# Moving a runtime branch ahead of the expert loop, and norms per tile behind it, in a two-layer mixer and mixture-of-experts kernel

## Chip, cores, metric

One core of a Trainium2 chip. The metric is the device time of one execution in microseconds (us).

## What is computed

Two layers over 512 tokens (256 context, 256 latent) of width 1024. Each layer has a token mixer and then a mixture of experts: every token goes to its best group of four and, in it, to the two best of eight experts, 32 experts in all, each a SwiGLU MLP with 256 hidden columns. Around the experts stands a residual with a layer norm, and the next layer begins with a second, plain norm of that result:

```python
for l in range(DEPTH):
    yc, yl = token_mixer(modulate(xc, sh1c, sc1c), modulate(xl, sh1l, sc1l), ...)
    xl = layer_norm(DEEPNORM_ALPHA * xl + g1l * yl, ln1_g[l], ln1_b[l])
    if not last:   # the context stream, in the same way
        xc = layer_norm(DEEPNORM_ALPHA * xc + g2c * hier_moe(modulate(xc, sh2c, sc2c), *moe_args), ln2_g[l], ln2_b[l])
    xl = layer_norm(DEEPNORM_ALPHA * xl + g2l * hier_moe(modulate(xl, sh2l, sc2l), *moe_args), ln2_g[l], ln2_b[l])
```

Layer 0 does this for four tiles of 128 tokens, layer 1 for the two latent tiles alone. The shifts, scales and gates (sh, sc, g) come from a matrix `w_ada` of 1024 x 6144 per layer, which the kernel calls `ada`, in three parts of 2048 columns.

## The kernel before

The kernel is written in a framework that orders the instructions of each engine itself, from a simulated timeline, and places the waits; only TensorE's order inside the expert loop is fixed by hand (`manual_schedule`). A conditional block (`tc.If`) is one unit for the engines that take part in it.

`moe(l)` (L1278 to L1537) runs in this order. `route` finds every token's two experts and how many experts have more than 64 tokens; `route_rows` writes this as rows. Each expert has one block of 64 token places; further blocks, for experts with more tokens, are counted in `cnt`. Experts are taken in pairs: `fetch(j)` finds on VectorE (DVE, `who`) which tokens sit in pair j and gathers their rows from DRAM with an indirect DMA of GpSimd (POOL, `gather`); `turn` transposes them on TensorE (PE); `up`, `hidden` and `down` are the MLP; `combine` puts the results back to the tokens with matmuls by a 0/1 matrix, multiplies by the gate on DVE (L1444) and adds to the residual `X` (L1447), on POOL or DVE.

Expert weights come through a ring of buffers of 1 MB (`wm`: 4 of the pool W and 7 or 9 of the pool W2, and in layer 1 one more), issued by SyncE (SP); a pair takes six.

In layer 0 one further block is computed always, after pair 3 (`extra(0, self.wm)`). For all others there is the branch: `nov` is loaded from `cnt` into registers of PE, ScalarE (ACT), DVE and POOL (L1478), and behind the experts stands a nest of `tc.If(nov > ob)` (L1520), each with an `extra`. With these inputs no engine goes into it in either layer: it is jumped over.

In layer 0 the drain of the last `combine` is followed by `self.drain(self.ada(1, 1, True))`, the second part of the next layer's `ada`, with 16 weight loads of 512 KB through the 4 buffers of pool W alone, then by the branch, then by the norms, in groups of two tiles: `ln_stats` (BATCH_NORM_STATS2 on DVE, L209, and an inverse root by Newton steps, L147 to L154), `affine` (L236, L237), and `ln_scale` for the next layer's norm. Then `mixer(1)` starts: loads of `w_in`, `ada(1, 2)`, and per tile the normalised `xn` (ACT, L486), its transposes (PE, L489), scale and shift `h` (L502, L504), a split into high and low parts (L505, L160), and matmuls (L196 to L198). In layer 1 the branch and the norms of two tiles end the kernel, and the output is stored from L1537.

## Time and profile before

| | us |
|---|---|
| median of 3 runs | 1450.9 (1450.35 to 1451.05) |
| the profiled execution | 1449.59 |
| its span, first to last instruction | 1447.8 |

| engine | busy us | share |
|---|---|---|
| PE (matmul) | 1294.9 | 89% |
| DVE | 800.6 | 55% |
| ACT | 436.4 | 30% |
| POOL | 388.9 | 27% |

The expert loops lie at 542 to 817 us (layer 0) and 1197 to 1425 us (layer 1). Busy time counts an instruction from its start to its end; matmuls are pipelined and their ends are modelled. Idle time in brackets is that of the engine ahead of an instruction, with what ended it. An engine's name with a q is its sequencer: branches, register loads, semaphores, DMA issues.

### The profile page before, as it was taken

What the parts mean: (1) busy time and instruction counts of PE and PEld (TensorE: products, weight loads), DVE (VectorE), ACT (ScalarE), POOL (GpSimd) and SP (SyncE); (2) the same over time, 40 slices, a digit from 0 to 9 for tenths busy, and PEclk for the clock granted to TensorE, in tenths of its full rate; (3) what the DMA queues carried; (4) which work ended last, traced back from release to release, by engine and by line L of the source; (5) the groups of instructions that cost most, each with busy time, mean ns of one, the idle gap of its engine ahead of it and who ended that gap; (6) DMA issues with size and microseconds to landing.
All of it is one profiled execution on the core that took longest, in us unless ns stands there. A gap on an engine that the chain in (4) does not pass through costs nothing. (4 is left out here: it accounts for less than half of the span.)

```text
span 1447.8 us, 19597 instructions
## 1 busy us (share of the span) xinstructions
PE 1294.9 (89%) x6839; PEld 833.9 (58%) x6839; DVE 800.6 (55%) x2205; ACT 436.4 (30%) x976; POOL 388.9 (27%) x395
## 2 busy tenths in 40 slices
PE   5899999999998829899999967999999739999994
PEld 1788866776876623445444405897978633444442
DVE  3646677543246955446653458568775763343325
ACT  3434344443340102112112006355554202221210
POOL 1410114110342303343432412111524401222222
PEclk9899999999999859999999979999999959999997
DMA  9624464211257568979999596412434687999993
GB/s 331 195 95 146 139 207 145 83 30 59 88 182 259 183 241 307 404 274 408 407 407 409 215 304 227 125 44 75 128 127 151 202 290 293 416 417 416 414 417 126
DMA packets 146031, 339.60 MB, mean 235 GB/s; under 512 B 21552, under 2 KB 67792, under 8 KB 145920
## 3 DMA queue, kind: packets, MB, share of 16 engines
q1 hardware_dynamic: 137376, 322.87, 61.0%
q0 software_dynamic: 6096, 10.05, 2.1%
q10 hardware_dynamic: 2448, 5.31, 1.1%
q8 instruction: 57, 0.93, 0.3%
q14 instruction: 54, 0.44, 0.1%
HBM read 344.62 MB, written 4.29 MB: 241 GB/s over the span
## 5 line engine op out<-in xcount | busy, mean ns | idle before, releaser
L1404 PE MATMUL ps_g<-we,xs 128*64 128x512 f32 x992 | 236.7, 604 | 3.1 <-DMA we<-in_w_e_up 3.0
L1447 POOL TENSOR_TENSOR X<-X,acc 128x512 f32<-128x512 f32 x102 | 134.6, 1343 | 111.5 <-DVE acc L1444 111.2
L160 POOL TENSOR_TENSOR wsl<-wc,wsh 128x512 fp32r<-128x512 f32 x55 | 73.6, 1340 | 329.7 <-ACT wsh L176 282.4
L1404 PEld LDWEIGHTS ps_g<-we,xs 128*64 128x64 f32 x992 | 74.5, 139 | 140.7 <-issue 134.9
L176 ACT ACTIVATE wsh<-wc 128x512 fp32r<-128x512 f32 x162 | 99.0, 628 | 152.4 <-PE ps_g L197 83.1
L160 DVE TENSOR_TENSOR wsl<-wc,wsh 128x512 fp32r<-128x512 f32 x107 | 86.8, 815 | 97.6 <-ACT wsh L176 86.4
L1408 DVE SCALAR_TENSOR_TENSOR si<-si,ws,ps_g 128x256 f32<-128x256 f32 (+1 forms) x33 | 15.8, 480 | 206.0 <-ACT si L1407 206.0
L1427 PE MATMUL ps_a<-we,hidT 128*64 128x512 f32 x496 | 124.7, 601 | 3.2 <-DMA we<-in_w_e_down 3.1
L196 PE MATMUL ps_g<-wsh,hTh 128*128 128x256 f32 x400 | 115.8, 292 | 5.9 <-ACT hTh L527 3.1
L1360 POOL DMA_INDIRECT xr<-h2d,ti x33 | 34.7, 1053 | 310.0 <-PE ps_t L1372 204.6
L198 PE MATMUL ps_g<-wsh,hTl 128*128 128x256 f32 x400 | 113.1, 286 | 4.0 <-DVE hTl L160 3.3
L196 PE MATMUL ps_g<-hTh,wsh 128*128 128x512 f32 (+1 forms) x320 | 112.8, 352 | 1.8 <-ACT tg L621 1.8
L197 PE MATMUL ps_g<-wsl,hTh 128*128 128x256 f32 x400 | 114.2, 287 | 0.0
L197 PE MATMUL ps_g<-hTl,wsh 128*128 128x512 f32 (+1 forms) x320 | 111.1, 347 | 0.0
L198 PE MATMUL ps_g<-hTh,wsl 128*128 128x512 f32 (+1 forms) x320 | 110.4, 345 | 0.0
L375 PE MATMUL ps_d<-wada,sT 128*32 128x512 f32 x380 | 76.6, 662 | 31.4 <-DMA wada<-in_w_ada 31.4
L1444 DVE TENSOR_TENSOR acc<-ps_d,g 128x512 f32<-128x512 f32 x108 | 73.9, 688 | 37.8 <-PE ps_d L1442 21.7
L1441 PE MATMUL ps_d<-yh,pmr 128*128 128x512 f32 (+1 forms) x200 | 83.4, 418 | 0.6 <-DVE acc L1444 0.4
L196 PEld LDWEIGHTS ps_g<-wsh,hTh 128*128 128x128 f32 x400 | 76.9, 193 | 12.1 <-ACT hTh L527 3.4
L1407 ACT ACTIVATE si<-ps_g 128x256 f32<-128x256 f32 (+1 forms) x33 | 12.7, 384 | 236.0 <-PE ps_g L1404 195.1
L1427 PEld LDWEIGHTS ps_a<-we,hidT 128*64 128x64 f32 x496 | 38.6, 138 | 77.5 <-issue 63.4
L1442 PE MATMUL ps_d<-yl,pmr 128*128 128x512 f32 (+1 forms) x200 | 79.6, 400 | 0.9 <-DVE yl L190 0.9
(394 smaller groups left out, 2664.0 us busy)
## 6 DMA issues: line engine op xcount, KB each, us to landing
we<-in_w_e_gate SPq DMA_DIRECT2D x124, 512.0 KB
we<-in_w_e_up SPq DMA_DIRECT2D x124, 512.0 KB
we<-in_w_e_down SPq DMA_DIRECT2D x124, 512.0 KB
wada<-in_w_ada SPq DMA_DIRECT2D x95, 512.0 KB
wc<-in_w_in SPq DMA_DIRECT2D x63, 512.0 KB
wc<-in_w_out SPq DMA_DIRECT2D x16, 512.0 KB
wc<-in_w_bo_mla SPq DMA_DIRECT2D x8, 512.0 KB
wc<-in_w_bo_mlstm SPq DMA_DIRECT2D x6, 512.0 KB
```

Source lines behind the costliest of these rows:

```text
L160: eng.tensor_tensor(out=out, in0=a, in1=b, op=OP.subtract)
L176: self.nc.scalar.activation(view(hi), src, AF.Copy)
L196: self.nc.tensor.matmul(out, lhsT=ah, rhs=bh, start=(i == 0), stop=False)
L197: self.nc.tensor.matmul(out, lhsT=ah, rhs=bl, start=False, stop=False)
L198: self.nc.tensor.matmul(out, lhsT=al, rhs=bh, start=False, stop=(i == n - 1))
L375: nc.tensor.matmul(ps[32 * c:32 * c + 32], lhsT=self.sT[:, kb], rhs=wt[c // 2][:, (c % 2) * 512:(c % 2) * 512 + 512], start=(kb == 0), sto ...
L1404: nc.tensor.matmul(p[64 * e:64 * e + 64], lhsT=xs[:, k, 64 * e:64 * e + 64], rhs=W[e, k // 4][:, :, k % 4], start=(k == 0), stop=(k == 7))
L1427: nc.tensor.matmul(p[64 * e:64 * e + 64], lhsT=hT_[:, c, 64 * e:64 * e + 64], rhs=W[e, c, h], start=(c == 0), stop=(c == 1))
L1441: nc.tensor.matmul(p, lhsT=lt, rhs=yh[h][0:m], start=(j == 0), stop=False)
L1442: nc.tensor.matmul(p, lhsT=lt, rhs=yl[h][0:m], start=False, stop=(j == len(parts) - 1))
L1444: nc.vector.tensor_tensor(out=a, in0=p, in1=g2[t // 2][h], op=OP.mult)
L1447: eng.tensor_tensor(out=X, in0=X, in1=a, op=OP.add)
```

## The change

The branch moves ahead of the expert loop, behind the first pair's `fetch`; the second pair's `fetch` comes behind it. What stands in it no longer uses the ring of weight buffers: `extra` without `new` takes 12 small `st` tiles, loaded by 20 indirect DMAs instead of six, and one of the gather buffers. The weight tables are indexed by k instead of by half (same loads, same matmuls). The late `ada(1, 1)` uses the expert ring `wm` (all 11 buffers of 1 MB), and so does the pair of norm vectors `ln2`. The last `combine` adds to the residual on DVE alone, in an instruction that also gives the row sum; the norms follow per tile, with the sum of squares from ACT (`stats`: Square with an accumulator) in place of the batch-norm statistics; the affine works on 1024 columns at once and gives the row sum for the second norm.

```diff
@@ load_indexed
-        def load_indexed(ob, new):
+        def load_indexed(ob, new=None):
...
+            if new is None:
+                for k in range(8):
+                    wt = self.st(name="wx")
+                    for i in range(2):
+                        part(wt[:, i * 256:i * 256 + 256], i, k * 256)
+                    W[0, k] = wt.rearrange("p (g n) -> p g n", g=2)
+                for c in range(2):
+                    for h in range(2):
+                        Wd[0, c, h] = self.st(name="wx")
+                        part(Wd[0, c, h], 2, c * 1024 + h * 512)
+                return W, Wd
@@ ada
             for c in range(2):
-                wt.append(self.w("wada"))
+            if late:
+                t = self.wm("wada")
+                wt = self.halves2(t)
@@ combine
-                    a = self.pm(name="acc") if final else ep.tile([128, 512], F32, tag="acc", name="acc", bufs=2)
+                    a = self.pm(name="acc") if sums else ep.tile([128, 512], F32, tag="acc", name="acc", bufs=2)
                     nc.vector.tensor_tensor(out=a, in0=p, in1=g2[t // 2][h], op=OP.mult)
                     X = self.X[t][:, hs]
-                    eng = nc.vector if final and h else nc.gpsimd
-                    eng.tensor_tensor(out=X, in0=X, in1=a, op=OP.add)
+                    if sums:
+                        nc.vector.scalar_tensor_tensor(X, a, 1.0, X, op0=OP.mult, op1=OP.add,
+                                                       accum_out=sums[t][:, h:h + 1])
+                    else:
+                        nc.gpsimd.tensor_tensor(out=X, in0=X, in1=a, op=OP.add)
@@ new
+        def stats(X, nm, eps):
+            v, a, r = (self.ss_tile([128, 2], x) for x in "var")
+            q, v, a, r = v[:, 1:2], v[:, 0:1], a[:, 0:1], r[:, 0:1]
+            xi[0] += 1
+            nc.scalar.activation(xrs[xi[0] % 3], X, AF.Square, bias=nm, accum_out=q)
+            nc.vector.tensor_scalar(v, q, 0.5 / D, 0.5 * eps, op0=OP.mult, op1=OP.add)
+            self.newton(r, v, a)
+            return r
@@ ahead of the expert loop
-        got = {j: fetch(j) for j in range(2)}
+        got = {0: fetch(0)}
         eng = mybir.EngineType
         nov = nc.values_load(cnt[0:1, 0:1], engines=(eng.PE, eng.Activation, eng.DVE, eng.Pool), min_val=0, max_val=16)
+        o0, om = (0, 8) if last else (1, 16)
+        def more(ob):
+            with tc.If(nov > ob):
+                extra(ob)
+                if ob + 1 < om:
+                    more(ob + 1)
+        more(o0)
+        got[1] = fetch(1)
@@ behind the expert loop
         self.drain(comb)
-        self.drain(combine(done, True))
+        sums = {t: sm([128, 3], "sum", bufs=n) for t in QT}
+        comb = combine(done, sums)
+        for t in QT:
+            for h in range(2):
+                next(comb)
+            X = self.X[t]
+            nm, s2 = self.ss_tile([128, 4], "mv")[:, 0:1], sums[t][:, 2:3]
+            nc.vector.tensor_scalar(nm, sums[t][:, 0:1], sums[t][:, 1:2], -1.0 / D, op0=OP.add, op1=OP.mult)
+            r = stats(X, nm, EPS / ALPHA ** 2)
+            nc.vector.scalar_tensor_tensor(X, X, nm, lg, op0=OP.add, op1=OP.mult)
...
+            nc.vector.scalar_tensor_tensor(X, X, r, lb, op0=OP.mult, op1=OP.add, accum_out=s2)
...
+            r = stats(X, nm, EPS)
+            nc.vector.tensor_tensor(out=nb, in0=nm, in1=r, op=OP.mult)
+            self.nlx[t] = (r, nb)
         if not last:
-            self.half = None
             self.drain(self.ada(1, 1, True))
             self.half = None
-        o0, om = (0, 8) if last else (1, 16)
-        def more(ob):
-            with tc.If(nov > ob):
-                extra(ob, self.w2)
...
-        more(o0)
-        G2 = 2
-        for ts in [QT[i:i + G2] for i in range(0, n, G2)]:
-            st = self.ln_stats([self.X[t] for t in ts], EPS / ALPHA ** 2)
...
```

## Rows read from the trace of the kernel before

**Rows 1.** Windows: length, busy PE, PEld, DVE, ACT, POOL; PEclk, DMA share, GB/s

```profile
817.50:826.00 8.50, 8.42 (x44) 5.81 (x46) 7.21 (x12) 0.60 (x1) 5.56 (x5) 1.00 0.00 1
826.00:845.00 19.00, 13.72 (x60) 1.89 (x52) 1.41 (x3) 0.00 (x0) 0.89 (x1) 0.91 0.94 320
851.00:875.00 24.00, 16.74 (x52) 2.04 (x48) 23.77 (x83) 2.78 (x5) 2.53 (x2) 0.70 0.88 315
875.00:895.00 20.00, 15.52 (x95) 11.68 (x96) 15.46 (x48) 14.98 (x32) 3.78 (x5) 0.85 0.76 242
895.00:1128.00 233.00, 228.64 (x1625) 199.42 (x1624) 155.19 (x436) 118.22 (x286) 71.35 (x94) 1.00 0.36 112
1234.00:1415.00 181.00, 178.62 (x831) 79.77 (x830) 63.58 (x179) 37.38 (x74) 43.02 (x35) 1.00 1.03 416
```

**Rows 2.** The branch's line, L1520: durations ns min/median/max, first and last start

```profile
L1520 PEldq COMPARE_BRANCH  x2: 3495/4186/4878, 843.9 to 1428.6; - x2
```

**Rows 3.** Timeline of DVE at layer 0's end: start, us, instruction, idle before

```profile
826.38 1.06 DVE L1447 TENSOR_TENSOR X<-X,acc 128x512 f32<-128x512 f32 x1
845.00 0.69 DVE L381 TENSOR_TENSOR bada<-ps_d,bada 128x512 f32<-128x512 f32 x1 [17.55 <-PE ps_d L375]
851.23 2.47 DVE L209 BATCH_NORM_STATS2 ln_st<-X 128x6 f32<-128x512 f32 x4 [5.55 <-DVEq L1520]
```

**Rows 4.** Groups of DVE, 800 to 900 us: busy us, mean ns, idle before

```profile
L209 DVE BATCH_NORM_STATS2 ln_st<-X 128x6 f32<-128x512 f32 x16 | 9.8, 680 | 5.5 <-DVEq L1520 5.5
L1447 DVE TENSOR_TENSOR X<-X,acc 128x512 f32<-128x512 f32 x4 | 3.2, 796 | 0.0
```

**Rows 5.** The ada matmuls: group of 817.5 to 895 us, and the timeline's first piece

```profile
L375 PE MATMUL ps_d<-wada,sT 128*32 128x512 f32 x128 | 34.7, 766 | 15.4 <-DMA wada<-in_w_ada 15.4
...
825.08 2.78 PE L375 MATMUL ps_d<-wada,sT 128*32 128x512 f32 x24
```

**Rows 6.** Timeline of SP's DMA issues at layer 0's end

```profile
826.21 10.69 SPq L371 DMA_DIRECT2D wada<-in_w_ada  x10
...
841.27 2.97 SPq L442 DMA_DIRECT2D wc<-in_w_in  x4
844.99 23.77 SPq L371 DMA_DIRECT2D wada<-in_w_ada  x16
```

**Rows 7.** Groups of ACT, 480 to 1447 us: Square with accumulator, and table loads

```profile
L977 ACT ACTIVATE junk<-qd 128x384 f32<-128x384 f32 x2 | 1.0, 524 | 0.1
...
L1407 ACT ACT_TABLE_LOAD x2 | 2.6, 1283 | 0.0
```

**Rows 8.** Timeline of PE at the start of the experts, layer 0, then layer 1

```profile
542.55 1.95 PE L1372 MATMUL ps_t<-ident,xr 128*128 128x128 f32 x8 [5.89 <-DMA xr<-h2d,ti]
544.43 8.73 PE L1404 MATMUL ps_g<-we,xs 128*64 128x512 f32 x32
553.09 1.15 PE L1372 MATMUL ps_t<-ident,xr 128*128 128x128 f32 x8
...
1196.73 1.95 PE L1372 MATMUL ps_t<-ident,xr 128*128 128x128 f32 x8 [5.07 <-DMA xr<-h2d,ti]
```

**Rows 9.** Layer 0's start: SP's first and first later weight load, POOL's gather, DVE's search

```profile
488.14 0.36 SPq L1302 DMA_DIRECT2D we<-in_w_e_gate  x1
549.76 0.33 SPq L1302 DMA_DIRECT2D we<-in_w_e_gate  x1
...
537.96 1.14 POOL L1360 DMA_INDIRECT xr<-h2d,ti  x1 [38.13 <-DVE ti L1359]
...
537.33 0.69 DVE L1392 SCALAR_TENSOR_TENSOR pb<-rows 128x512 f32<-128x512 f32 x1 [0.23 <-ACT rows L1264]
```

**Rows 10.** Timeline of DVE at the kernel's end

```profile
1431.25 0.97 DVE L1447 TENSOR_TENSOR X<-X,acc 128x512 f32<-128x512 f32 x1
1434.67 2.47 DVE L209 BATCH_NORM_STATS2 ln_st<-X 128x6 f32<-128x512 f32 x4 [2.46 <-DVEq L1520]
1441.88 2.74 DVE L237 SCALAR_TENSOR_TENSOR X<-X,ln_r,ln 128x512 f32<-128x512 f32 x4
```

More of the change, by code (lines that the diff above doesn't have):

```diff
@@ L358, in bias @@
         def bias():
-            bt = (self.u(name="bada") if first else self.w("bada")[:, 0:512])
+            bt = self.pm(name="bada") if late else (self.u(name="bada") if first else self.w("bada")[:, 0:512])
             for c in range(4):
@@ L1333, in load_indexed @@
                 for i in range(2):
-                    part(wt[:, i * 1024:i * 1024 + 1024], i, c)
-                W[0, c] = wt.rearrange("p (g k n) -> p g k n", g=2, k=4)
+                    part(wt[:, i * 1024:i * 1024 + 1024], i, c * 1024)
+                wv = wt.rearrange("p (g k n) -> p g k n", g=2, k=4)
+                for k in range(4):
+                    W[0, 4 * c + k] = wv[:, :, k]
             wt = new("wx")
             for c in range(2):
-                part(wt[:, c * 1024:c * 1024 + 1024], 2, c)
+                part(wt[:, c * 1024:c * 1024 + 1024], 2, c * 1024)
                 for h in range(2):
@@ L1502, in moe @@
         finish(hid)
-        ln2 = []
-        for nm in ("ln2_g", "ln2_b"):
-            if not ln2:
-                wt = self.wp.tile([128, 2 * D], F32, tag="W", name="ln2", bufs=self.NW)
-            v = wt[:, len(ln2) * D:(len(ln2) + 1) * D]
-            nc.sync.dma_start(out=v, in_=I[nm][l].partition_broadcast(128))
-            ln2.append(self.halves(v))
-        lg, lb = ln2
-        self.drain(comb)
-        self.drain(combine(done, True))
+        ln2 = self.wm("ln2")
+        for i, nm in enumerate(("ln2_g", "ln2_b")):
+            nc.sync.dma_start(out=ln2[:, i * D:i * D + D], in_=I[nm][l].partition_broadcast(128))
@@ new lines, in moe @@
+        lg, lb = ln2[:, 0:D], ln2[:, D:2 * D]
+        self.drain(comb)
+        sums = {t: sm([128, 3], "sum", bufs=n) for t in QT}
[8 more added lines that the diff above has]
+            nc.vector.scalar_tensor_tensor(X, X, nm, lg, op0=OP.add, op1=OP.mult)
+            if last:
+                for h in range(2):
+                    hs = slice(h * 512, h * 512 + 512)
+                    nc.vector.scalar_tensor_tensor(X[:, hs], X[:, hs], r, lb[:, hs], op0=OP.mult, op1=OP.add)
+                    nc.sync.dma_start(out=self.out[0, (t - 2) * 128:(t - 1) * 128, hs], in_=X[:, hs])
+                continue
+            nc.vector.scalar_tensor_tensor(X, X, r, lb, op0=OP.mult, op1=OP.add, accum_out=s2)
+            self.dump(f"x2_{l}_{t}", X)
+            nm, nb = self.ss_tile([128, 4], "mv")[:, 0:1], self.ss_tile([128, 1], "nb")
+            nc.vector.tensor_scalar(nm, s2, -1.0 / D, None, op0=OP.mult)
+            r = stats(X, nm, EPS)
+            nc.vector.tensor_tensor(out=nb, in0=nm, in1=r, op=OP.mult)
+            self.nlx[t] = (r, nb)
@@ L1513, in moe @@
         if not last:
-            self.half = None
             self.drain(self.ada(1, 1, True))
             self.half = None
-        o0, om = (0, 8) if last else (1, 16)
-        def more(ob):
-            with tc.If(nov > ob):
-                extra(ob, self.w2)
-                if ob + 1 < om:
-                    more(ob + 1)
-        more(o0)
-        G2 = 2
-        for ts in [QT[i:i + G2] for i in range(0, n, G2)]:
-            st = self.ln_stats([self.X[t] for t in ts], EPS / ALPHA ** 2)
-            for t, (mean, r) in zip(ts, st):
-                X2 = self.halves(self.X[t])
-                self.affine(X2, X2, mean, r, lg, lb, last or str(t) in F3)
-                self.dump(f"x2_{l}_{t}", self.X[t])
-                if not last:
-                    self.nlx[t] = self.ln_scale(self.X[t])
-                else:
-                    for h in range(2):
-                        nc.sync.dma_start(out=self.out[0, (t - 2) * 128:(t - 1) * 128, h * 512:h * 512 + 512], in_=X2[h])
```

34 lines of the change are left out of this document (20 added, 14 removed).

## The prediction

> **What bounds the kernel now.** The shares of the engines come first: PE is busy 89% of the span, so time is to be had only where PE waits. The windows show where that is [rows 1]. From 895 to 1128 us, the second mixer, PE is busy for 228.6 of 233 us: PE bounds it. From 1234 to 1415 us, the experts of layer 1, the DMA engines are busy throughout (share 1.03) at 416 GB/s: weight transfers bound it. Between 817.5 us, where layer 0's last expert matmuls end, and 895 us lie 77.5 us in which neither holds. PE looks busy there for 8.42 + 13.72 + 16.74 + 15.52 = 54.4 us of the four windows, but 34.7 of that are the 128 matmul records of the two `ada` parts [rows 5], stretched by waits inside; the first 24 of them, whose data was there, took 2.78 us, so 128 cost 14.8 us at that pace. PE's real work in the 77.5 us is about 54.4 - 34.7 + 14.8 = 34.5 us. This handover is what the change can shorten, and then the end of the kernel, where PE does nothing.
>
> The DVE timeline shows the handover's order [rows 3]. DVE ends the last residual add at 826.38 + 1.06 = 827.4, waits 17.55 us for PE's `ada(1, 1)` to add a bias at 845.00, then 5.55 us more at the branch, and starts the norms at 851.23 us. From there it is full (23.77 of 24 us, then 15.46 of 20) [rows 1], and the mixer's first matmuls follow it. `ada(1, 1)` is late because its weights are: SP could issue ten of the sixteen loads only from 826.21 us on, when buffers of pool W came free [rows 6], while no DMA moved anything from 817.5 to 826 us [rows 1]. So the chain is: four buffers, `ada`, the bias add, the branch, the norms, the mixer.
>
> **The change, part by part. Handover of layer 0.** DVE's work between 817.5 and 895 us is 7.21 + 1.41 + 23.77 + 15.46 us [rows 1] plus the bias add of 0.69 [rows 3], 48.5 us. Removed are 16 batch statistics, 9.8 us; added are the four residual adds that POOL did, at the price of DVE's own four, 3.2 us [rows 4]. That leaves 41.9 us of work in a stretch of 77.5 (the affine is the same number of elements, the Newton steps are as many). Upper end: the norm of tile 0 starts at its second residual add and DVE never waits, so it is done about 2 us of first wait after 817.5 + 41.9, at 861 us: a gain of 34. Lower end: the scheduler still puts the `ada` bias add ahead of the norms on DVE; then only the branch's 5.55 us and 9.8 - 3.2 = 6.6 us of work go: 12. The norms no longer need `ada` for anything, and the branch is gone, so they can start where the adds end, at 827.4 + 3.2 = 830.6 instead of 851.2: 20.6 us from the start alone, and the 6.6 us of lighter work on top would give 27. I take 23, because three things give some of it back. The sum of squares is a trip to ACT: a Square with accumulator of 384 columns takes 0.524 us [rows 7], so 1024 take at most 1.40 (by proportion) twice per tile, eight in all, 11 us on ACT, which was busy for only 18.4 us of the four windows; the trip is hidden behind the next tile's adds except for the last tile. Next, the transfers: up to 895 us the DMA engines left idle 8.5 us in the first window, 1.1, 2.9 and 4.8 in the others (by their shares), 17 us in all, so a gain far above 17 needs `ada(1, 1)` to be loaded before 826, which the 11 buffers allow, and `w_in` not to be pushed behind `ada(1, 2)`, whose 16 loads still go through pool W, of which `ln2` now as before holds a buffer. Last, the first mixer tiles lie in memory that the norms still use (`xr` takes the squares), so the mixer may have to wait for the last tile's norm. `ada`'s matmuls stay, 14.8 us on PE, in time that PE has. If ScalarE needs its table changed for Square after the experts' Silu, that is one load of 1.28 us [rows 7], inside the bound.
>
> **The end.** DVE's last add ends at 1431.25 + 0.97 = 1432.2 us, the branch costs 2.46 us, and the norms run from 1434.67 to 1441.88 + 2.74 = 1444.6 us [rows 10]. Gone are 2.46 us and four batch statistics, 2.47 us. Added are two adds from POOL (1.6 us at rows 4's 0.80) and, for the second tile, the Square's trip of up to 1.4 us, with DVE working on the first tile's affine meanwhile. Between 1 and 5 us, I take 3: the removed time is on the path, the added only in part. The stores behind it are unchanged.
>
> **The branch at its new place.** It stands in PE, ACT, DVE and POOL behind the first `fetch`. What it costs there is not in the trace; what it cost behind the experts is. PE's jump took 3.5 and 4.9 us [rows 2], DVE was held 5.55 and 2.46 us [rows 3, 10]. In layer 0, PE was idle for 5.89 us ahead of 542.55 us, waiting for the first gather; in layer 1 for 5.07 us [rows 8]. PE's jump of at most 4.9 us fits into either. DVE's last search pass for pair 0 ends around 538 us [rows 9]; 5.55 us later it is 543.6, and the first expert matmul, whose PSUM buffer the branch's DVE work also uses, started at 544.43: still covered. Behind DVE's jump is queued the search for pair 1: four passes of 0.69 us, up to 546.4; the gather for pair 0 took 542.55 - 537.96 = 4.6 us from POOL's issue to PE, so pair 1 is there at about 551.5, and PE asked for it at 553.09. So the cover is thin, 0.8 to 1.6 us, and if it fails PE itself waits, and with it the release of weight buffers. Per layer: between 0 (all covered) and 5.55 (DVE's hold wholly on the path); nothing there becomes shorter. I take 0.5 each, 1 in all, nearest to the rows of PE's idle time. SP takes no part in the branch. Of what stands behind it in the code, SP issued `w_in` and `ada(1, 2)` at 841.27 and 844.99 us, before DVE came out of it [rows 3, 6], so SP doesn't stop. If the weight loads of the first pairs go behind SP's loads of the gate rows, they lose the head start of 488 us, but nothing waited for them until 544 us, and SP's queue then stood still up to 549.76 [rows 9]: cost nothing, unless they wait for the branch itself (a rival). The 20 indirect DMAs on POOL are not issued when the branch is jumped over.
>
> **A rule that speaks against it.** The row is that a jump costs PE 3.5 to 4.9 us wherever it stands [rows 2]. [...] By this rule the stall is moved and not removed, and the nest of further blocks, now longer, is jumped over all the same; the gain of 26 would lose some 5 us in each layer. This is rival 1.
>
> **Sum.** 23 + 3 - 1 = 25 us less. The profiled execution of 1449.6 us (span 1447.8 and 1.8 around it) becomes 1424.6; it stands 1.3 us below the median of the runs, so the median of 1450.9 becomes 1426.
>
> **Rivals.** Rival 1: *the branch stays a stall at its new place*: PE's or DVE's hold is not covered, since the gather of pair 1 comes behind both. For it: the cover is under 2 us. Against: PE's idle time ahead of the first pair. At about 5 us per layer: 1450.9 - 26 + 10 = 1435. Rival 2: *the norms don't move up*: the order found for DVE or the memory shared with the mixer keeps them behind `ada`, and only the branch and the statistics go. 1450.9 - 12 - 3 + 1 = 1437. For it: in the trace DVE did wait for the bias with nothing else. Against: all it could have done there stood behind the branch. Rival 3: *the weight loads wait for the branch* (slower): if SP's expert loads are put behind it, nothing is loaded when the first pair starts. In layer 1 fourteen buffers, 14.7 MB, which were loaded ahead, would be read in the loop that the transfers bound, at 416 GB/s 35 us; in layer 0, which starts with four buffers of 1.05 MB for pair 0, 10 us before the first matmul can run. Together 45 us against gains of 26: 1470. It decides as soon as more than 26 us of transfers (10.8 MB) move behind the branch. Against it: SP issued past the branch [rows 6].
>
> **How the numbers follow.** Forecast 0.66, with its own range from 1411 (gains of 34 and 5, rounded down) to 1434; rival 1 0.12, rival 2 0.14, rival 3 0.06; 0.02 are left. Range 1411 to 1440: the forecast with rivals 1 and 2. A measurement of this kernel can tell 0.2%, some 3 us. Faster: forecast and rivals 1 and 2, less a little for their tails, 0.91; slower: rival 3, 0.06; same 0.03.
>
> **What would show it.** Right: in the DVE timeline the first norm of layer 0 starts within some 6 us of the end of layer 0's experts and ahead of the `ada` bias add; SP issues the sixteen `ada` loads without a gap; from the end of layer 0's experts to the mixer's full stretch about 54 us instead of 77.5; PE's branch lies inside the wait for the first gather; from the last add to the end of the kernel about 3 us less. Wrong: PE waiting for the gather of pair 1; weight loads issued only after the branch; the first mixer copy waiting for the last Square; or a mixer that is longer, since the two branches now enclose all of it and the scheduler's order inside can change.

## The result, and the profile after

The changed kernel takes 1433.3 us (median of 4 runs, 1433.11 to 1435.75), the kernel before 1450.8 us beside it: a ratio of 0.9888 with a 95% interval of 0.9873 to 0.9903, and 17.5 us by the medians. The profiled execution took 1433.49 us (span 1431.7). The prediction was 1426 (1411 to 1440): faster, inside its range, with 17.5 of the 25 us it named.

| stage, profiled executions | before, us | after, us | difference |
|---|---|---|---|
| start to the first expert matmul of layer 0 | 544.43 | 545.41 | +1.0 |
| from there to layer 0's last `down` (start of each) | 269.52 | 269.02 | -0.5 |
| end of layer 0's experts to the last modulated row of mixer 2 | 350.10 | 333.80 | -16.3 |
| that row to the router's copy behind ScalarE's store | 7.44 | 3.22 | -4.2 |
| router and first gather of layer 1 | 21.65 | 21.58 | -0.1 |
| first row transpose of layer 1 to its first expert matmul | 1.87 | 3.11 | +1.2 |
| first expert matmul to the second run of weight loads | 4.22 | 5.83 | +1.6 |
| weight stream of layer 1, to the last `down` | 219.45 | 223.90 | +4.5 |
| last `down` to the end | 25.53 | 22.26 | -3.3 |
| span | 1447.8 | 1431.7 | -16.1 |

The windows of the changed kernel from the end of layer 0's experts on (length, busy PE, PEld, DVE, ACT, POOL; PEclk, DMA share, GB/s), against [rows 1]:

```profile
818.00:826.00 8.00, 7.84 (x32) 5.33 (x30) 6.74 (x15) 1.48 (x2) 0.08 (x1) 1.00 0.86 345
826.00:845.00 19.00, 12.93 (x81) 2.71 (x80) 16.08 (x54) 6.42 (x13) 1.95 (x3) 0.82 0.56 183
845.00:866.00 21.00, 11.16 (x44) 2.30 (x45) 14.66 (x52) 10.21 (x18) 2.41 (x2) 0.76 0.75 279
866.00:889.31 23.31, 23.15 (x156) 19.04 (x157) 15.64 (x33) 16.51 (x36) 8.14 (x8) 1.00 0.89 281
889.31:1115.00 225.69, 220.02 (x1561) 191.52 (x1560) 151.90 (x425) 113.91 (x279) 68.56 (x91) 0.99 0.37 115
1217.00:1400.00 183.00, 179.55 (x820) 77.62 (x818) 63.18 (x178) 36.94 (x73) 42.80 (x35) 1.00 1.03 407
```

PE is full from 866 us on, where it was full only from 895. But two windows of 19 and 21 us remain in which it is busy for 12.93 and 11.16 us. And the last row has 407 GB/s, where the kernel before had 416.

The DVE timeline at layer 0's end, against [rows 3] (start, us, instruction; the first norm's mean, the last residual add, the bias of `ada`):

```profile
824.88 0.21 DVE L1560 TENSOR_SCALAR ln_mv<-sum 128x1 f32<-128x1 f32 x1
...
830.56 0.68 DVE L1469 SCALAR_TENSOR_TENSOR X<-acc,X 128x512 f32<-128x512 f32 x1
...
841.27 0.69 DVE L387 TENSOR_TENSOR bada<-ps_d,bada 128x512 f32<-128x512 f32 x1
```

The norms begin at 824.88 us, ahead of the last adds and of the bias, instead of 851.23. PE's `ada` in the same stretch, against [rows 5]:

```profile
826.15 7.07 PE L381 MATMUL ps_d<-wada,sT 128*32 128x512 f32 x64
836.71 5.70 PE L381 MATMUL ps_d<-wada,sT 128*32 128x512 f32 x16 [3.49 <-DMA wada<-in_w_ada]
852.81 4.97 PE L381 MATMUL ps_d<-wada,sT 128*32 128x512 f32 x16 [10.40 <-DMA wada<-in_w_ada]
```

All 64 matmuls of `ada(1, 1)` now run in one go: their weights lay there. The next ones, of `ada(1, 2)`, wait 3.49 and 10.40 us. SP issues their sixteen loads in one run of 29 us, against 23.77 in [rows 6]:

```profile
831.27 29.00 SPq L377 DMA_DIRECT2D wada<-in_w_ada  x16
```

ScalarE's last Square and the first copies of the mixer:

```profile
858.93 1.15 ACT L1480 ACTIVATE xr<-X,ln_mv 128x1024 f32<-128x1024 f32 x1 [4.76 <-DVE ln_mv L1572]
...
860.08 4.32 ACT L492 ACTIVATE xn<-X,ln_nb,ln_r 128x512 f32<-128x512 f32 x6
```

What no part of the prediction had is the step of 4.2 us behind the mixer. ScalarE issues the last two stores of the normalised rows (`h2d`) before it can copy for the router. ScalarE's timeline there, first in the kernel before (start, duration, instruction, idle time ahead):

```profile
1168.42 6.55 ACTq L743 DMA_DIRECT2D h2d<-h  x2
1175.08 1.08 ACT L263 ACTIVATE h2T<-ps_a 128x512 f32<-128x512 f32 x2 [12.26 <-DMA h2d<-h]
```

The same two in the changed kernel:

```profile
1152.58 2.33 ACTq L749 DMA_DIRECT2D h2d<-h  x2
1155.02 1.09 ACT L263 ACTIVATE h2T<-ps_a 128x512 f32<-128x512 f32 x2 [8.04 <-PE ps_a L261]
```

The issue took 6.55 us before and 2.33 after. In both, SP issues four expert loads and four halves of a `down` about then; before, they began 0.6 us ahead of the store, after, 4.5 us ahead. The four halves, before and after:

```profile
1169.93 2.55 SPq L1318 DMA_DIRECT2D we<-in_w_e_down  x4
```

```profile
1150.05 3.27 SPq L1326 DMA_DIRECT2D we<-in_w_e_down  x4
```

The traces of all fourteen kernels agree on this step. It is 6.4 to 7.4 us long in three of them (the kernel before, e2 and e12) and 2.3 to 3.6 in the other eleven. ScalarE's second store always leaves 1.3 to 2.5 us behind the last of these four issues, and in those three kernels alone that issue ends 3.4 to 3.7 us behind the last modulated row, elsewhere at most 0.4 us behind it. So the step goes with the place of SP's loads. That is read from the traces; no run was made to test it.

The end of the kernel, against [rows 10] (last add, last affine):

```profile
1419.50 0.68 DVE L1469 SCALAR_TENSOR_TENSOR X<-acc,X 128x512 f32<-128x512 f32 x1
...
1426.67 1.42 DVE L1566 SCALAR_TENSOR_TENSOR X<-X,ln_r,ln 128x512 f32<-128x512 f32 x2
```

### The profile page after: what moved, and what is told of

Its sections match the earlier page's. It is cut to its first block, busy times and chain, and to the rows that moved or that the text cites. A ratio compares the mean times of both kernels' runs of the same rounds, so it can differ in the third digit from the quotient of the medians.

```text
span 1431.7 us, 19677 instructions
## 1 busy us (share of the span) xinstructions
PE 1290.5 (90%) x6839; PEld 832.9 (58%) x6839; DVE 798.3 (56%) x2197; ACT 450.0 (31%) x998; POOL 379.9 (27%) x389
## 5 line engine op out<-in xcount | busy, mean ns | idle before, releaser
L1426 PE MATMUL ps_g<-we,xs 128*64 128x512 f32 x992 | 240.1, 609 | 6.5 <-DMA we<-in_w_e_up 4.2
L1472 POOL TENSOR_TENSOR X<-X,acc 128x512 f32<-128x512 f32 x96 | 125.1, 1326 | 110.2 <-DVE acc L1466 110.2
L381 PE MATMUL ps_d<-wada,sT 128*32 128x512 f32 x380 | 69.1, 641 | 30.4 <-DMA wada<-in_w_ada 15.4
L1429 ACT ACTIVATE si<-ps_g 128x256 f32<-128x256 f32 (+1 forms) x33 | 12.7, 384 | 241.5 <-PE ps_g L1426 186.4
```

The lines of the kernel that those rows point to most:

```text
L381: nc.tensor.matmul(ps[32 * c:32 * c + 32], lhsT=self.sT[:, kb], rhs=wt[c // 2][:, (c % 2) * 512:(c % 2) * 512 + 512], start=(kb == 0), sto ...
L1426: nc.tensor.matmul(p[64 * e:64 * e + 64], lhsT=xs[:, k, 64 * e:64 * e + 64], rhs=W[e, k], start=(k == 0), stop=(k == 7))
L1472: nc.gpsimd.tensor_tensor(out=X, in0=X, in1=a, op=OP.add)
```

## The experiments

Each was timed against the kernel before on the same chip, so the ratios compare; a ratio of 0.001 is 1.45 us. The changed kernel itself stands at 0.9888 (0.9873 to 0.9903).

| run | median, us | ratio to before (95%) | against the changed kernel, us |
|---|---|---|---|
| e1_squares_apart | 1432.9 | 0.9894 (0.9868 to 0.9920) | +0.9 |
| e2_xn_st | 1440.6 | 0.9945 (0.9926 to 0.9964) | +8.3 |
| e3_silu_first | 1432.7 | 0.9895 (0.9869 to 0.9922) | +1.0 |
| e4_no_branch | 1424.6 | 0.9837 (0.9810 to 0.9865) | -7.4 |
| e5_branch_only | 1439.1 | 0.9912 (0.9898 to 0.9926) | +3.5 |
| e6_align_layer1 | 1430.0 | 0.9862 (0.9844 to 0.9879) | -3.8 |
| e7_align_all | 1426.4 | 0.9827 (0.9811 to 0.9843) | -8.8 |
| e8_ada12_early | 1428.6 | 0.9836 (0.9821 to 0.9850) | -7.5 |
| e9_old_norms | 1432.8 | 0.9869 (0.9849 to 0.9888) | -2.8 |
| e10_ada_in_w | 1508.3 | 1.0404 (1.0382 to 1.0427) | +74.9 |
| e11_combined | 1422.7 | 0.9802 (0.9786 to 0.9817) | -12.5 |
| e12_combined_xn | 1428.3 | 0.9846 (0.9826 to 0.9866) | -6.1 |

The last column is the difference of the ratios times 1450.8. Where the intervals of two ratios overlap, as those of e1, e3, e5, e6 and e9 do with the changed kernel's, the difference isn't clear of noise. A stage that is the same code in two kernels also differs between their profiled executions: layer 0's experts, first matmul to last `down`, took 268.8 to 271.6 us in the kernels that leave them and their buffers alone.

### Does the mixer wait for the norms' memory? e1 and e2

In e1 the Squares write into tiles of their own, so that `xr` is free earlier:

```diff
-            nc.scalar.activation(xrs[xi[0] % 3], X, AF.Square, bias=nm, accum_out=q)
+            nc.scalar.activation(self.cp.tile([128, D], BF16, tag="st", name="sq", bufs=self.NST), X, AF.Square, bias=nm, accum_out=q)
```

> The changed kernel, with the Squares of the norms writing to the constant pool (the st tiles) instead of xr, which lies in the memory of the expert stage. In the changed kernel the first xn copy of the mixer starts at 860.08 us, right behind the last Square (858.93 to 860.17), though its norm's nb was ready at 838.76. Theory S (the copy waits because its tile lies on the xr that the Squares write): the copies come forward as soon as the Squares write elsewhere, and up to 11.7 us are won (the stretch from the last norm to the Exp table of the mixer took 25.5 us in the changed kernel and 13.75 in the one before): about 1422 to 1426. Theory E (the copy's tile lies on other memory of the expert stage that is in use until the last norm, such as ln2 or sums): nothing moves, 1431 to 1436. In the list of ScalarE's instructions of this kernel the copies still stand behind the last Square, which speaks for E.

Theory S falls. The Squares write elsewhere, and the copies still start right behind the last of them:

```profile
855.37 1.15 ACT L1480 ACTIVATE sq<-X,ln_mv 128x1024 bf16<-128x1024 f32 x1 [4.82 <-DVE ln_mv L1572]
...
857.03 4.32 ACT L492 ACTIVATE xn<-X,ln_nb,ln_r 128x512 f32<-128x512 f32 x6
```

In e2 the mixer's copies `xn` get tiles outside the memory that the expert stage used:

```diff
-                xn = (self.u if l else self.st)(name="xn")
+                xn = self.st(name="xn")
```

> The changed kernel, with one word different: the xn copies of the second mixer go to st tiles of the constant pool (as in the first mixer) instead of u tiles of the mixer's pool, which is laid over the expert stage's memory. Theory M (the copies waited for memory of the expert stage, and with them transposes, modulation and the mixer's first matmuls): the first xn copy starts soon after nb of tile 0 or 1 (838.8 to 851 us), ahead of the last Squares; the stretch from the last norm to the mixer's Exp table shrinks from 25.5 us towards the 13.75 of the kernel before: 6 to 12 us faster, 1421 to 1427. Rival D (the norms' chain on DVE to 862.25 us and ada(1, 2), whose matmuls stand among the transposes on PE and waited 10.4 us for their loads until 852.81, set the end whatever the copies do): the copies come earlier and the mixer starts less than 3 us earlier, 1430 to 1434.

Here the first copy starts at 846.22 us, before the Squares of the last tiles. So here it was the place of the copies' own tiles, in memory of the expert stage, that had put them behind. But nothing is won: the mixer's Exp table is loaded at 887.23 us instead of 887.73, and the kernel is 8 us slower. PE's waits from the end of layer 0's experts to 888 us (what, for what: us in total, times, longest), first this kernel, then the changed one:

```profile
PE ps_t L495 <- ACT xn L492: 9.3, 2, 7.6
PE ps_d L381 <- DMA wada<-in_w_ada: 5.2, 2, 3.8
```

```profile
PE ps_d L381 <- DMA wada<-in_w_ada: 14.5, 5, 10.4
```

The wait only changes its name: 14.5 us for the loads of `ada(1, 2)` become 5.2 us for them and 9.3 for copies, because PE's transposes now stand ahead of most of these matmuls. Rival D holds for the start of the mixer, though not for the time it named (1430 to 1434). The profiled execution is 6.8 us longer. The last tile's norm came 6.4 us later (868.48 instead of 862.09, with the experts' end 0.6 us later), as the copies and their modulation now stand between the norms on DVE and ScalarE; mixer 2 ended 2.3 us later in its stretch; and the step behind ScalarE's store was 6.9 us long instead of 3.2, as in the kernel before. So the larger part is that step, which the copies' memory was not expected to touch.

### What does the branch cost at its new place? e3 and e4

The changed kernel behind the branch in layer 0: ScalarE, then PE, then DVE.

```profile
543.47 1.28 ACT L1396 ACT_TABLE_LOAD   x1 [6.91 <-PE ps_t L1394]
544.76 1.08 ACT L1396 ACTIVATE xs<-ps_t 128x512 f32<-128x512 f32 x2
545.87 1.28 ACT L1429 ACT_TABLE_LOAD   x1
```

```profile
542.29 1.94 PE L1394 MATMUL ps_t<-ident,xr 128*128 128x128 f32 x8 [6.37 <-DMA xr<-h2d,ti]
545.41 8.97 PE L1426 MATMUL ps_g<-we,xs 128*64 128x512 f32 x32 [1.18 <-ACT xs L1396]
554.32 1.15 PE L1394 MATMUL ps_t<-ident,xr 128*128 128x128 f32 x8
```

```profile
541.60 0.69 DVE L1414 SCALAR_TENSOR_TENSOR pb<-rows,iot 128x512 f32<-128x512 f32 x1 [4.12 <-DVEq L1517]
```

DVE is held 4.12 us, and PE's jump (3.6 and 4.0 us in the two layers) lies inside its wait for the gather, as the prediction had it; PE doesn't wait for the gather of pair 1 at 554.32. But ScalarE loads a table of 1.28 us ahead of its first copy, and PE waits 1.18 us for that copy. The kernel before has one load per layer, behind the copies:

```profile
545.15 1.28 ACT L1407 ACT_TABLE_LOAD   x1
```

In e3 a small Silu behind the branch is to load the table early:

```diff
         more(o0)
+        warm = sm([128, 1], "warm", bufs=1)
+        nc.scalar.activation(warm, self.zeros, AF.Silu)
         got[1] = fetch(1)
```

> The changed kernel, with one Silu of a single element on ScalarE right behind the branch. In the changed kernel ScalarE loads its table twice behind the branch in each layer: 1.28 us ahead of the first xs copy (543.47 us) and again ahead of the first Silu (545.87 us); the kernel before loaded it once. Theory T (the load ahead of the copy is on the path to the first expert matmul, which came 0.98 us later than before though the rows came 0.26 us earlier): with the one Silu the table is loaded during the wait for the first gather, the copy has none ahead of it and the first Silu neither; in layer 0 and layer 1 about 1.2 us each, or 2.5 in all: 1430 to 1431.5. Rival C (the weight stream sets the pace of the expert loop and eats what its first matmul gains): within 0.7 us, 1432.6 to 1434.

It tells nothing on theory T. The scheduler put the Silu ahead of the branch, where nothing holds it, and both loads are still there (541.91 and 544.30 us), with two more ahead of the branch (499.85 and 515.03 us); the time is that of the changed kernel. In e11 the Silu reads a row buffer that the branch writes: there one load of 1.28 us stands at 544.25 us, and in layer 0 the first expert matmul comes 2.68 us behind the first row transpose instead of 3.12, so that 0.4 of the 1.2 us is back. In layer 1 it comes 3.42 us behind instead of 3.11, so nothing is won there.

Kernel e4 has no branch, so that further expert blocks are never computed:

```diff
-        more(o0)
```

> The changed kernel without the branch and the blocks behind it (further expert blocks are left out; the inputs here never enter them). What the branch costs at its new place. Theory B (it holds DVE for 4.1 and 3.2 us and makes ScalarE load its table a second time; the first expert matmul is 1.0 to 1.2 us later for it): 1.2 to 1.7 us per layer, 1429.5 to 1431. Rival H (all of it lies within the wait for the first gather or is made up by the weight stream): within 0.7 us, 1432.6 to 1434. Should it be 5 us per layer, which is the price that the prediction's first rival named, it would be 1423.

The first expert matmul comes 1.88 us behind the first transpose in both layers, as before: theory B's 1.24 us per layer is the table. But the kernel is 7.4 us faster than the changed one, not 2.5. Most of the rest is in the weight stream of layer 1, and it is no wait: in the middle of that stage (windows of 180 us; the last column is GB/s) the changed kernel moves 408, the one without the branch 416.

```profile
1219.00:1399.00 180.00, 176.55 (x808) 76.69 (x806) 62.76 (x177) 36.61 (x72) 40.80 (x34) 1.00 1.03 408
```

```profile
1212.00:1392.00 180.00, 177.47 (x821) 78.80 (x821) 63.34 (x178) 36.95 (x73) 42.88 (x35) 1.00 1.03 416
```

### Why 408 instead of 416 GB/s? e6 and e7

With the moved blocks the nine buffers of W2 in layer 1 begin at byte 155456 of each partition. Without the branch and in the kernel before they begin at 148224, a multiple of 256. Of the 7232 bytes between, 64 come from two small tiles that the blocks add, and these 64 take the start off the multiple. The addresses are those of the framework's allocation; no trace shows them.

In e6 one of the small tiles is taken from a pool that is there already, so that layer 1's buffers move by 64 bytes:

```diff
-                v = sm([128, 3], nm + sfx, bufs=1 if sfx else 4)
+                v = self.ss_tile([128, 4], "mv")[:, 0:3] if sfx else sm([128, 3], nm, bufs=4)
```

> The changed kernel, with the two 12-byte tiles that the moved blocks add (tkx, wsx) taken from the ring of the norms' small tiles. Nothing else is different, but the nine weight buffers of layer 1 (W2) begin 64 bytes earlier in each partition: at byte 155392 instead of 155456. In the kernel before and in the one without the branch they begin at 148224. Of these, 148224 and 155392 are multiples of 256 and 155456 isn't. Theory A (the address of the buffers sets the rate: 416 GB/s for multiples of 256, 408 else): slices of layer 1's experts at 416 GB/s, about 4.4 us less than the changed kernel, 1428 to 1430. Rival B (the branch ahead of the loop does it, by its code or by the order it leaves): 408 GB/s, 1432 to 1434.

In e7 layer 0's and pool W's buffers are moved as well:

```diff
-        th = self.sm([128, 2, 8], "th")
+        th = self.sm([128, 2, 8], "th", bufs=1)
+        self.cp.tile([128, 8], F32, name="pad")
...
+        sm([128, 8 if not last else 24], "pad", bufs=1)
         xi = [0]
```

> As the kernel with layer 1's buffers aligned, and the other weight buffers too: the four of pool W (77920 to 77824) and layer 0's seven of W2 (170112 to 169984) begin at multiples of 512. By theory A (address) the experts of layer 0, which run at 401 to 408 GB/s in all kernels so far, run at 416 as well: some 4 us less again in the 200 us from 570 to 810 us where the transfers are the bound, 1423 to 1426; if a multiple of 256 that is not one of 512 were what counts, layer 0 would stay at 408. By rival B no slice changes, 1432 to 1434.

The second diff stands on top of the first. Theory A holds, twice. With layer 1's buffers at 155392 its stage runs at 415 GB/s, with the branch in place; the stream of 223.90 us becomes 220.23, and the kernel is 3.8 us faster by ratios whose intervals overlap. With layer 0's and pool W's buffers at multiples of 512 as well, layer 0 follows, which had run at 407 or 408 in every kernel so far; from the first expert matmul to the last `down` it takes 266.9 instead of 269.0 us. The rate is the firm part of this: e11 and e12, whose layer 0 is aligned in the same way, run at 413 and 416 there too, but take 268.7 and 270.5 us for that stage, about as long as kernels without it. First e6 and e7 in layer 1, then the kernel before, the changed kernel and e7 in layer 0:

```profile
1214.00:1394.00 180.00, 177.46 (x823) 79.61 (x823) 64.27 (x180) 37.47 (x75) 44.29 (x36) 1.00 1.03 415
```

```profile
1210.00:1390.00 180.00, 177.90 (x829) 81.24 (x830) 64.70 (x180) 38.04 (x75) 44.38 (x36) 1.00 1.02 417
```

```profile
670.00:770.00 100.00, 100.00 (x482) 50.15 (x482) 54.37 (x116) 20.19 (x40) 41.99 (x34) 1.00 1.03 408
```

```profile
670.00:770.00 100.00, 100.00 (x480) 50.26 (x480) 55.08 (x118) 20.36 (x40) 41.38 (x34) 1.00 1.03 408
```

```profile
670.00:770.00 100.00, 100.00 (x477) 48.86 (x477) 52.16 (x109) 18.69 (x37) 41.62 (x33) 1.00 1.03 415
```

The addresses of W2 that ran fast are 148224, 155392 (multiples of 256) and 169984 (of 512); those that ran slow leave 64 or 128 over 256. The four buffers of pool W stood 96 bytes over (77920) in e6, whose layer 1 ran at 415; with them aligned as well, in e7, it ran at 417. Slow against fast is 408 against 416 GB/s, or 2%; why the start address does this, no run here shows.

### Which part of the change brought the gain? e5, e9, e10

Kernel e5 is the kernel before with the branch moved, together with the small tiles that its blocks now use; the residual adds, the norms and the loads of `ada(1, 1)` are as in the kernel before:

```diff
-        got = {j: fetch(j) for j in range(2)}
+        got = {0: fetch(0)}
...
+        more(o0)
+        got[1] = fetch(1)
...
             self.drain(self.ada(1, 1, True))
...
-        more(o0)
```

> The kernel before, with the branch alone moved (and the blocks behind it in their new form); sums, norms and ada as before. Theory P (the prediction's terms): DVE's hold of 5.55 us in layer 0 and 2.46 us in layer 1 behind the experts goes, 0.5 us per layer is paid at the new place: about 7 us less than the kernel before. Theory W (what the traces of the changed kernel and of the one without the branch show at the new place): 1.2 us per layer for ScalarE's second table load, and the weight stream of layer 1 runs at 408 instead of 416 GB/s, 4.4 us over its 200 us: 5.55 + 2.46 - 2.4 - 4.4 = about 1 us less than the kernel before, and the profile shows 408 GB/s in the slices of layer 1's experts.

Both theories fall, on the low side: 12.7 us by the medians (1451.8 to 1439.1), though layer 1 runs at 407 GB/s as theory W said. The DVE timeline of this kernel shows why:

```profile
822.95 1.27 DVE L209 BATCH_NORM_STATS2 ln_st<-X 128x6 f32<-128x512 f32 x2
...
846.87 0.69 DVE L383 TENSOR_TENSOR bada<-ps_d,bada 128x512 f32<-128x512 f32 x1 [1.04 <-DMA wc<-in_w_in]
```

The old norms, with batch statistics, start at 822.95 us between the residual adds, and the bias of `ada(1, 1)` follows at 846.87. In the kernel before, the branch stood behind `ada` and ahead of the norms, and every instruction of the norms stayed behind it. So the branch's price at its old place was not only the 5.55 us for which it held DVE, but also what it kept in order: the norms behind the bias. In time that is less than the 12.7 us. The profiled execution of this kernel is 9.2 us shorter than that of the kernel before. The stretch from layer 0's experts through mixer 2 is 8.8 us shorter and the end of the kernel 2.9, and the step behind ScalarE's store is 4.4 shorter (3.0 us), which neither theory counted; against that stand 5.6 us more in layer 1's experts and 1.2 for the table there.

Kernel e9 is the changed kernel with the old residual adds and the old norms, in groups of two tiles; `ada(1, 1)` keeps the eleven buffers of the expert ring:

```diff
-        comb = combine(done, sums)
...
-            r = stats(X, nm, EPS / ALPHA ** 2)
...
+        self.drain(combine(done, True))
...
+        for ts in [QT[i:i + G2] for i in range(0, n, G2)]:
+            st = self.ln_stats([self.X[t] for t in ts], EPS / ALPHA ** 2)
```

> The changed kernel with the norms of the kernel before (batch statistics on DVE, POOL's share of the last adds, norms over pairs of tiles); the branch at its new place and ada(1, 1) over the ring of eleven buffers stay. From the end of layer 0's experts to the first weight load of layer 1 the kernel before took 313.6 us, the one with the branch alone moved 304.8, the changed one 297.2. Theory R (the 7.6 us between the last two are the ring's: PE's 64 matmuls of ada(1, 1) took 7.07 us in one go once their weights lay there): about 297 to 299 us in that stretch, and a time within 2.5 us of the changed kernel. Theory S (they are the sums', the Squares' and the norms' per tile): 303 to 305 us, 5 to 8 us slower than the changed kernel.

Theory R holds: 297.4 us to the first weight load of layer 1, and a time that can't be told from the changed kernel's. The stretch from the end of layer 0's experts to the last modulated row of mixer 2, in the kernel before, with the branch alone (e5), with the branch and the ring (e9), with everything, and with `ada(1, 2)` early:

```profile
817.54:1167.64 350.10, 311.89 (x1986) 243.96 (x1984) 238.54 (x655) 144.27 (x336) 100.00 (x119) 0.94 0.49 156
```

```profile
817.60:1158.89 341.29, 312.26 (x1986) 244.61 (x1984) 241.55 (x654) 144.43 (x336) 100.13 (x119) 0.95 0.50 162
```

```profile
818.20:1153.68 335.48, 302.81 (x1986) 244.47 (x1984) 240.70 (x654) 143.97 (x336) 99.82 (x119) 0.95 0.48 157
```

```profile
818.00:1151.80 333.80, 302.32 (x1986) 242.96 (x1984) 237.23 (x646) 153.21 (x352) 94.19 (x115) 0.95 0.49 158
```

```profile
822.00:1150.91 328.91, 301.43 (x1986) 243.29 (x1984) 233.68 (x647) 153.62 (x352) 94.34 (x115) 0.97 0.50 160
```

350.1, 341.3, 335.5, 333.8, 328.9: the branch 8.8, the ring 5.8, the new norms 1.7. Each is one execution, so a step of 1.7 tells little. All five rows have the same 1986 matmuls, and PE's busy time falls from 312 to 301-303 us with the ring, since the matmuls of `ada(1, 1)` no longer stretch over their loads.

Kernel e10 was to have the new norms with the old loads of `ada(1, 1)`:

```diff
-            if late:
-                t = self.wm("wada")
-                wt = self.halves2(t)
-            else:
-                wt = [self.w("wada") for c in range(2)]
+            wt = [self.w("wada") for c in range(2)]
```

> The mirror image: the changed kernel, with ada(1, 1) loaded through the four buffers of pool W as before, and its bias there; the branch moved and the new norms stay. Theory R (the ring is worth the 7.6 us): 303 to 305 us from the end of layer 0's experts to layer 1's first weight load, 5 to 8 us slower than the changed kernel. Theory S (the norms are): within 2.5 us of the changed kernel.

Inconclusive: 75 us slower, by a fault of the edit. Half a buffer of pool W that the first mixer had left over was handed to `ada(1, 1)` at the end of layer 0, and so was kept through its experts; the kernel before drops such a half first. SP's first load of `ada(1, 1)` writes into the tile with the old name:

```profile
859.54 1.06 SPq L373 DMA_DIRECT2D bada<-in_w_ada  x1
```

What the ring is worth therefore rests on e9 against e5 alone.

### What bounds the handover now? e8, e11, e12

In e8 `ada(1, 2)` leaves the mixer and follows `ada(1, 1)` through the ring of eleven buffers:

```diff
-            ada0 = self.ada(1, 2)
+            ada0 = iter([None] * 8)
...
             self.drain(self.ada(1, 1, True))
+            self.drain(self.ada(1, 2, True))
```

> The changed kernel, with ada(1, 2) drained behind ada(1, 1) at the end of layer 0, over the same ring of eleven buffers, instead of among the first copies of the second mixer with the four of pool W. In the changed kernel PE waits 14.5 us in the handover for the loads of ada(1, 2), 10.4 of them in one piece to 852.81 us, and its transposes stand behind these matmuls. Theory Q (the four buffers are still the bound of the handover, now for ada(1, 2)): PE's wait goes, and the mixer's Exp table comes 8 to 12 us earlier: 1422 to 1426. Rival N (the norms' chain on DVE, to 862 us, with the copies behind it, takes its place at once): the wait turns into one for xn, within 3 us of the changed kernel, 1430 to 1434.

7.5 us faster than the changed kernel by the ratios, whose intervals don't touch. In the handover PE waits 13.5 us instead of 14.5 + 1.5, in other places:

```profile
PE ps_t L495 <- DVE h L510: 5.6, 1, 5.6
PE ps_d L381 <- DMA wada<-in_w_ada: 5.3, 15, 1.1
PE ps_t L495 <- ACT xn L492: 2.6, 1, 2.6
```

So both hold in part, and the time lies between the two that were expected: of the 14.5 us for loads 9.2 are gone, but the modulation and the copies now take 8.2 us, 6.7 more than before. The Exp table came 64.8 us behind the experts' end instead of 69.7, 5 us of the 8 to 12 expected; the same 4.9 us stand at the end of the mixer (rows above). The profiled execution was only 0.8 us shorter than the changed kernel's, as layer 0's experts began 2.7 us later in it, ahead of anything that was changed.

Kernel e11 joins e6, e7 and e8, and adds a Silu behind the branch that reads a buffer of the rows:

```diff
+        warm = self.ss_tile([128, 4], "mv")[:, 0:1]
+        nc.scalar.activation(warm, xrs[2][:, 0:1], AF.Silu)
```

> The changed kernel with three things that the runs so far speak for: all weight buffers at multiples of 256 bytes, ada(1, 2) behind ada(1, 1) over the ring, and one single-element Silu on ScalarE behind the branch that reads a row buffer written in the branch, so that it can't be put ahead of it. If their gains add up (6.9 and 5 us against the kernel before, and 1.2 us per layer for the table): about 14 us less than the changed kernel, 1419 to 1421. If the wait for ada(1, 2) and the faster stream eat each other's gain, 1423 to 1427. That the Silu does its work is to be seen in the trace: first expert matmul 1.9 instead of 3.1 us behind the first transpose of the rows.

1422.7 us, 28 less than the kernel before and 12.5 less than the changed one by the ratios. That lies between the two expectations, and both kernels are beaten. The Silu did its work in layer 0 only (above).

The edit of e2 on top of e11:

> The combined kernel, with the xn copies in st tiles besides. Alone, that made the changed kernel some 7 us slower: PE then waited 9.3 us for copies instead of 14.5 for ada(1, 2). Theory Q2 (with the wait for ada(1, 2) gone the copies are what PE waits for, 2.6 us for xn and 5.6 for the modulation in the kernel with ada(1, 2) early): 3 to 6 us less than the combined kernel. Rival N2 (the copies' ScalarE and DVE work pushes the last tiles' norms back, as it did alone, by 6.4 us): same as the combined kernel or up to 7 us slower.

5.6 us slower than e11 by the medians, the time that rival N2 named, but not for its reason. The copies did not come forward here; the first still stands behind the last Square (859.09 us) and the last tile's `nb` (862.25):

```profile
862.32 2.92 ACT L493 ACTIVATE xn<-X,ln_nb,ln_r 128x512 f32<-128x512 f32 x4
```

From the end of layer 0's experts the norms take as long as in e11 (41.1 us to the last `nb`), and so does the stretch to the last modulated row (328.8 and 328.7 us). What is longer is the step behind ScalarE's store, 6.4 instead of 2.3 us, as in e2. So neither theory is tested by this run.

## Why the prediction was right, and where it was wrong

**The sum.** It was 23 + 3 - 1 = 25 and the profiled execution gave 16.1. The end is 3.3 where 3 was said. The handover with its mixer gave 16.3 where 23 was said. The branch cost 1.2 us of table per layer and 4.5 us of stream, and with the 1.6 us at the start of layer 1's experts that is 8.5 where 1 was said. The step behind ScalarE's store gave 4.2 that were not in the sum. 16.3 + 3.3 + 4.2 - 8.5 = 15.3; the rest is 0.2 us ahead of layer 0's experts, 0.5 in them and 0.1 in the router. So the gain was sized too high and the cost too low, and a help that nobody counted made up for part of both. Without that help, which is luck, the time would have been about 1437.5: still in the range, but outside the forecast's own (to 1434) and where rival 2 stood.

**The step that failed: the handover's 23.** The prediction put it together as 20.6 us from an earlier start, 6.6 us of lighter work on DVE, and about 4 us given back. The start was 26.3 us earlier (824.88 instead of 851.23). The 6.6 us of work went, nearly, but not the time. From the first norm to the last tile's `nb` DVE was busy for 36.74 of 36.75 us before and for 31.13 of 37.37 after, in both with some other work between (length, then busy PE, PEld, DVE and so on, as in the windows above):

```profile
851.23:887.98 36.75, 27.69 (x122) 9.92 (x119) 36.74 (x123) 11.51 (x23) 6.29 (x6) 0.76 0.93 319
```

```profile
824.88:862.25 37.37, 22.39 (x119) 5.25 (x119) 31.13 (x105) 13.76 (x24) 4.36 (x4) 0.77 0.62 217
```

The 5.6 us that DVE works less it waits more. The prediction had the trip to ScalarE "hidden behind the next tile's adds except for the last tile"; it isn't. DVE waits for ScalarE's Squares, and the Newton steps, taken tile by tile, follow one another where two tiles used to alternate. The group of the Squares' readers, with its idle time:

```profile
L1481 DVE TENSOR_SCALAR ln_v<-ln_v 128x1 f32<-128x1 f32 x8 | 1.2, 153 | 4.9 <-ACT xr L1480 4.9
```

Run e9 says the same in time: with the old norms the kernel is as fast. And of the 26.3 us of earlier start 10 were given back, not 4. PE waits 14.5 us for the weights of `ada(1, 2)`. The prediction named those sixteen loads through pool W, but priced them only by the DMA engines' idle time; the limit is the four buffers, as it had been for `ada(1, 1)`, and it was moved by one step and not removed (e8: 4.9 us in the mixer's end). That the first copies would wait for the last Square was foreseen as well, and came (860.08 behind 858.93), but e2 shows that it isn't what bounds.

**The right time for a partly wrong reason.** "The norms no longer need `ada` for anything, and the branch is gone" put two causes into one term. Run e5 parts them: the norms never needed `ada`; the branch kept them behind it. Moving it alone is 12.7 of the 17.5 us, with the loss of stream and table already taken off, but with the 4.4 us of the store's step in it; in the handover and its mixer it is 8.8 us of 16.3. The ring for `ada(1, 1)` is 5.8 us by the stretches and 6.2 by the ratios (0.9912 to 0.9869); it had no term of its own. The sums, Squares and norms per tile are between a gain of 1.7 us by the stretches and a loss of 2.8 us by the ratios, whose intervals overlap: not to be told from nothing.

**The branch at its new place.** The prediction bounded it by 0 and 5.55 us a layer and took 0.5. All that it listed as cover held: PE's jump inside the wait for the gather, DVE's 4.12 and 3.20 us without a wait of PE for pair 1. (Its 551.5 us for the rows of pair 1 is 551.0 by its own terms, 546.4 + 4.6; nothing hangs on it.) It asked for a table load in the wrong place, behind the experts for the Square, where there is none (the next there is the Exp's, at 887.73 us); the load came behind the join. The block behind the join begins with a load of 1.28 us (543.47 us), though ScalarE had run Copy without one ahead of the branch, for the `rows` at 534.49 and 535.96 us. Behind the old place none was loaded; ScalarE's copies there start at once, and the next load is that of the Exp at 901.73 us:

```profile
851.23 2.19 ACT L176 ACTIVATE wsh<-wc 128x512 fp32r<-128x512 f32 x4 [32.95 <-DVEq L1520]
```

What decides whether such a block begins with a load, no run here shows. The 4.5 us of the stream are a cost of the small tiles that came with the branch. No row of the kernel before could show them, but the two rates stood in its own trace: 408 GB/s in layer 0, 416 in layer 1.

**The rivals.** Rival 1 (the stall isn't covered) is refuted in its mechanism: the stall is covered. Its 10 us are near to the 7.4 that e4 gives for the branch at its new place, by table and addresses. Rival 2 (the norms don't move up) is refuted by 824.88. Rival 3 (weight loads wait for the branch) is refuted by SP, which issues the first load of layer 0's experts at 487.87 us, against 488.14 in [rows 9]. What the prediction weighed against the move, that the jump costs PE as much at its new place, came: it takes 3.6 and 4.0 us on PE there, against the 3.5 and 4.9 of [rows 2], and DVE is held for 4.12 and 3.20. It changed nothing in the time, because both holds found cover.

**What would show it.** First norm early and ahead of the bias: yes. Sixteen `ada` loads without a gap: yes for `ada(1, 1)`. 54 us from the experts' end to the mixer's full stretch instead of 77.5: it is 48 (818 to 866), but `ada(1, 2)` is part of that full stretch; by the mixer's Exp table it is 69.7 instead of 84.2. About 3 us less from the last add to the end: 12.2 instead of 16.6 from its start, 4.4 less, of which the stage as a whole kept 3.3.

## What to carry to other kernels

Price a branch by what its place keeps in order, and not by its stall alone: list what stands behind it that needs nothing ahead of it. When work leaves an engine, ask whether the engine will then wait instead. When a wait for loads is taken away by giving them more buffers, look for the next loads that still go through the few; here the wait moved there (14.5 us of PE, for `ada(1, 2)`). When a change adds even a small tile, compare the start addresses of the streamed buffers before and after: here a remainder of 64 or 128 over 256 bytes cost 2% of a stream that was the bound (408 against 416 GB/s).

## What the runs showed of the hardware that was not expected

The rate of the weight loads follows the start address of the buffers of W2: 413 to 417 GB/s at multiples of 256 bytes, 407 or 408 else, in the middle of the stage, in both layers of the kernel before, the changed one and eleven of the twelve others, and in layer 1 of e10 (its layer 0, at 309, isn't bound by the stream). ScalarE loads a table of 1.28 us behind the branch ahead of the experts, which isn't entered, ahead of a plain copy, and a second one for the Silu 1.1 us later; behind the same branch at its old place it loads none. An issue of two stores on ScalarE's queue takes 2.33 us or 6.55 us in the same program position, in step with where a run of SP's loads stands (not tested), and the router behind it waits that long.
